# Weight tiles at 128 instead of 64 bytes into their places, and 16 slots that begin 128 bytes later

## The chip, the cores and the metric

The kernel runs on one core of one Trainium2 chip. The metric is the device time of one execution in microseconds (us), the median of several runs; lower is better. Engines are named as in the profile: PE is TensorE's matmul and PEld its weight load, DVE is VectorE, ACT is ScalarE, POOL is GpSimd and SP is SyncE, which here only starts transfers.

## The reference

A decoder trunk of two layers over 512 positions of width 1024, float32 throughout. Layer 0 mixes tokens by retention, layer 1 by an mLSTM; both are followed by a gated feed-forward block with a short causal convolution. Cut to what matters:

```python
def conv_ffn(h, w_up, conv_w, conv_b, w_down):
    u = causal_dwconv(h @ w_up, conv_w, conv_b)
    a, b = jnp.split(u, 2, axis=-1)
    return (jax.nn.silu(a) * b) @ w_down

for i in range(2):
    h = rmsnorm(x, norm_tok_g[i]) * (1.0 + sc_t) + sh_t      # sc, sh, gt from c @ ada_w
    y = retention_mixer(...) if i == 0 else mlstm_mixer(...)   # 4 heads, keys 256, values 512
    x = x + gt_t * y
    h = rmsnorm(x, norm_ffn_g[i]) * (1.0 + sc_f) + sh_f
    x = x + gt_f * conv_ffn(h, ...)                            # inner width 2816
return rmsnorm(x, final_g)
```

Nearly all of the work is matrix products of the 512 positions with weights: the mixers' input and output projections, and the feed-forward block's two.

## The kernel before

**Operands in two parts.** Each float32 operand of a product is split into a high part, rounded to the float32r format, and a low part that holds the rest. A product is three matmuls: high by high, high by low, low by high. So the names come in pairs: `whi` and `wlo` for weights, `hh` and `hl` for the normed input h, `t24h` and `t24l` and `t3h` and `t3l` for sums of its parts, `ggh` and `ggl` for the gated values of the feed-forward block, `yh` and `yl` for a mixer's output, `qkh` and `mqkh` (with an l) for queries and keys, `vh` and `vl` for values, `sh` and `sl` for scores.

**Products.** A matmul loads one operand of 128 columns into the array (PEld) and streams the other through it, 256 or 512 columns wide; while one is streamed the next is loaded. The results are named by their use: `p` are the folded projections, which form four quarter products by seven half-size ones (`fold_pairs`, `folded`), 256 columns wide; `pv` are values, where the input is loaded and the weights are streamed, 256 wide when folded and 512 wide in the first head of each layer; `psc` are scores (keys loaded, queries streamed), `pav` is scores by values (values loaded, scores streamed); `po` are output and down projections, 512 wide, but 256 wide in `boundary`, where a layer half ends and the next one's norm begins; `pf` are the first projections after a norm, 256 wide; `pms` are the means of squares for a norm. `pp` are plain projections, 512 wide.

**Places.** On-chip memory is taken from pools. The pool `slots` has 62 places of 128 partitions by 512 float32 (2,048 bytes each in a partition); all activations lie there. The pool `wpool` has 18 places of 1,024 + `WPAD` float32 (4,352 bytes each) for weights. `WPAD = 64` leaves room for a tile to begin later than its place: tiles of folds, of boundaries and of `ones_d`, which a norm's sums are multiplied with, begin `OFF` float32 into the place (`[:, OFF : OFF + WCOLS]`), those of plain projections begin at 0. `OFF` is 16, which is 64 bytes. In `Beside`, the down projections' weights between the folds, only the last of four low parts is put `OFF` further. A place of `slots` and a place of `wpool` begin alike by 256 bytes: both sizes and the pools' starts are multiples of that.

**Order of the work.** Every instruction is first written down as a call (`Plan.add`), with an estimate of its time and a due time worked back from TensorE's order. `Plan.run` then goes through the engines' clocks and picks for each engine the call that is due first and can start. A tile gets its place when its first writer is picked: the pool's free places are kept in a list sorted by the time at which the place came free, and the first is taken (`room[b.key].pop(0)[1]`). A tile that takes a place over waits on the chip for the last reader of the one before. `Plan.issue` issues everything in this order, so all rows of the profile carry its line, L387, and have to be told apart by their tiles.

**Streams and stages.** Weights come from DRAM by SP's transfers; ACT writes the high part; the low part comes either from DVE (a subtraction) or from ACT and a transfer on POOL that adds (`wlo<-ws`, `wlo<-wt`, `wlo<-raw`). ACT and DVE also read the products out of PSUM, split them, and do the convolutions and norms. The stages by time: conditioning and first projections to about 85 us, retention heads to about 370, boundary and first projections to about 430, feed-forward block to about 705, boundary to about 765, mLSTM heads to about 1090, boundary to about 1150, feed-forward block to about 1430, and the last boundary.

Of the kernel before, what the change touches and what calls it, by code (L numbers as in the profile page):

```python
# [10 lines left out]
F32 = mybir.dt.float32  # L11
F32R = mybir.dt.float32r
# [4 lines left out]
P = 128  # L17
T = 512
# [18 lines left out]
LANDING = (2.5, 3.0)  # L37
LEAD = (4.0, 4.5)
WPAD = 64
OFF = 16  # L40
DIRECT = (0, 0)
ROOT_AT = 1
SPLIT = 4
# [3 lines left out]
NSLOTS = 62  # L47
# [46 lines left out]
class Buf:  # L94


    def __init__(self, pool, shape, dt, tag, name, bufs, psum=False):
        self.args, self.shape, self.key, self.bufs, self.psum = (pool, shape, dt, tag, name), shape, tag, bufs, psum
        self.real, self.uses, self.log, self.at = None, 0, [], ""

    def get(self):
        if self.real is None:
            pool, shape, dt, tag, name = self.args
            self.real = pool.tile(shape, dt, tag=f"{tag}{self.at}", name=name)
        return self.real

# [46 lines left out]
class Plan:  # L153
# [114 lines left out]
    def run(self):  # L268
# [5 lines left out]
        room = {key: [(0.0, i) for i in range(n)] for key, n in KINDS.items()}  # L274
# [32 lines left out]
        def choose(e):  # L307
            cand = []
            for due, n in wait[e]:
                t = start_of(n, free[e])  # L310
                if t is not None:
                    cand.append((due, n, t))
                    if len(cand) == 40:
                        break
            if not cand:
                return None
            soonest = min(t for _, _, t in cand) + 0.02
            for due, n, t in cand:
                if t > soonest:
                    continue  # L320
                end = t + calls[n].occ

                if e == "PE" or not any(d < due and t < t2 < end and d + lag - end < HURRY for d, _, t2 in cand):
                    return t, e, n
            t, n = min((t, n) for _, n, t in cand if t > soonest)
            return t, e, n

        best = {e: choose(e) for e in engines}
        while len(out) < len(calls):
            if not any(best.values()):  # L330
                held = [(calls[n].eng, calls[n].name, [b.args[4] for b in calls[n].bufs])
                        for e in engines for _, n in wait[e][:4]]
                live = [(b.args[4], b.uses) for b in {id(b): b for c in calls for b in c.bufs}.values()
                        if b.bufs and b.log is None and b.uses]
                print(len(live), live)
                raise RuntimeError(f"{len(out)} of {len(calls)}: {[b.args[4] for b in calls[pe[pe_at]].bufs]} {held}")
            t, e, n = min(c for c in best.values() if c)
            c, dirty = calls[n], {e}
            for b in c.bufs:
                if b.log is not None:  # L340
                    b.log, b.busy = None, 0.0
                    if b.bufs:
                        b.at = room[b.key].pop(0)[1]
                        dirty.update(engines)
                        makers[b.key].remove(b.maker)
            occ = c.occ
            if e == "POOL" and c.shared:
                port = (t, t + occ)
            elif e == "DVE" and c.shared:
                occ += SHARE * max(0.0, min(t + occ, port[1]) - max(t, port[0]))  # L350
            if c.fn and c.fn != table:
                table, occ = c.fn, occ + 1.3
            wait[e].remove((c.due, n))
            if e == "PE":
                issued.add(n)
                while pe_at < len(pe) and pe[pe_at] in issued:
                    pe_at, lag = pe_at + 1, t - calls[pe[pe_at]].due
            free[e] = t + occ
            if c.dma:
                dma_free = max(dma_free, t + occ + 1.2) + c.dma  # L360
                c.end = dma_free + LANDING["accum_op" in c.k]
            else:
                c.end = t + occ + c.lat
            for b in c.bufs:
                b.busy = max(b.busy, c.end)
                b.uses -= 1
                if not b.uses and b.bufs:
                    insort(room[b.key], (b.busy, b.at))
                    dirty.update(engines)
            for m, real in c.succs:  # L370
                s = calls[m]
                s.left -= 1
                s.ready = max(s.ready, c.end if real else t + occ)
                if not s.left:
                    dirty.add(s.eng)
                    insort(wait[s.eng], (s.due, m))
            out.append(n)
            self.log.append((t, n, occ))
            for d in dirty:
                best[d] = choose(d)  # L380
# [10 lines left out]
def trunk(ctx: ExitStack, tc: tile.TileContext, xT, cb, pos, vec, ident, decay, zmask, ada, w_s0, w_in0, w_v0,  # L391
          w_o0, w_in1, w_v1, w_f1, w_o1, w_up, w_dn, out):
    nc = tc.nc
    const = ctx.enter_context(tc.tile_pool(name="const", bufs=1))
    slots = ctx.enter_context(tc.tile_pool(name="slots", bufs=1))
    wpool = ctx.enter_context(tc.tile_pool(name="wpool", bufs=1))
    asides = ctx.enter_context(tc.tile_pool(name="asides", bufs=1))
    cond = ctx.enter_context(tc.tile_pool(name="cond", bufs=1))
# [6 lines left out]
    def uid(s):  # L405
        count[0] += 1
        return f"{s}_{count[0]}"

    def tile_of(pool, shape, dt, tag, name):
        return Buf(pool, shape, dt, tag, name, KINDS.get(tag, 0), tag == "ps")  # L410

    def slot(s, dt=F32, w=T):
        return tile_of(slots, [P, w], dt, "s", uid(s))

    def wide(s, dt=F32):
        return tile_of(wpool, [P, WCOLS + WPAD], dt, "w", uid(s))
# [7 lines left out]
    def fixed(pool, shape, dt, name):  # L424
        b = tile_of(pool, shape, dt, name, name)
        b.get()
        return b

    plan = Plan()
    V, A, G, PE, S = (plan.engine(*p) for p in (("DVE", nc.vector), ("ACT", nc.scalar), ("POOL", nc.gpsimd),  # L430
                                                ("PE", nc.tensor), ("SP", nc.sync)))

    V.memset(fixed(const, [P, 32], F32, "pad")[:], 0.0)
    ones = {}
    for name, v in (("d", 1.0 / D), ("v", 1.0 / DV), ("1", 1.0)):
        off = OFF if name == "d" else 0
# [78 lines left out]
    class Chunk:  # L517
        def __init__(self, src, n, off, added=False):
            self.off, self.added = off, added
            self.raw = wide("raw")[:, off : off + n]  # L520
            S.dma_start(self.raw, src)
# [122 lines left out]
                self.p[name] = hi, low_by(name in VADDED)(raw[r], hi, OFF)  # L644

    class Pair:
        def __init__(self, s, w=T):
            self.hi, self.lo = slot(s + "h", F32R, w), slot(s + "l", F32R, w)

        def split(self, src, r=slice(None), eng=None):  # L650
            A.copy(self.hi[:, r], src)
            (eng or V).tensor_tensor(self.lo[:, r], src, self.hi[:, r].bitcast(F32), op=ALU.subtract)

    def pair_of(s, src):
        p = Pair(s)
        p.split(src)
        return p

# [343 lines left out]
    def center_split(v, ps):  # L1002

        t, m = slot("vt"), tile_of(cols, [P, 1], F32, "vm", uid("vm"))
        tf = t[:]
        A.activation(tf, ps[:], AF.Copy, accum_out=m[:])
        G.tensor_scalar(m[:], m[:], -1.0 / DV, None, op0=ALU.mult)
        p = Pair("v")
        A.activation(p.hi[:], tf, AF.Identity, bias=m[:])
        V.scalar_tensor_tensor(p.lo[:], tf, m[:], p.hi[:].bitcast(F32), op0=ALU.add, op1=ALU.subtract)  # L1010
        v.append(p)

    def plain_split(v, ps):
        p = Pair("v")
        p.split(ps[:])
        v.append(p)

# [531 lines left out]
        A.activation(k[:], k[:], AF.Square)  # L1549
        G.tensor_scalar(cos[:], k[:], -2.0, 1.0, op0=ALU.mult, op1=ALU.add)  # L1550

    def rope(p1, p2):
        t = [slot("rp")[:] for _ in range(4)]
        V.tensor_tensor(t[0], p1[:], cos[:], op=ALU.mult)
        V.tensor_tensor(t[1], p2[:], sin[:], op=ALU.mult)
        V.tensor_tensor(t[2], p1[:], sin[:], op=ALU.mult)
        V.tensor_tensor(t[3], p2[:], cos[:], op=ALU.mult)
        V.tensor_tensor(t[0], t[0], t[1], op=ALU.subtract)
        V.tensor_tensor(t[2], t[2], t[3], op=ALU.add)
        return [pair_of("qk", t[n]) for n in (0, 2)]  # L1560

    def half_pair(st, name, finish):

        got = []

        def then(ps):
            got.append(ps)
            if len(got) == 2:
                st[name] = finish(*got)
        return then  # L1570

    h0 = []
# [262 lines left out]
    def conv_then(i, name, kt):  # L1835
        ch = (0 if name == "q" else 8) + i * 2 + kt

        def then(ps):
            acc = slot("mc")[:]
            c = lambda j: col("mcw", j * 16 + ch)  # L1840
            A.activation(acc, ps[:], AF.Identity, bias=col("mcb", ch), scale=c(3))
            for j, s in ((2, 1), (1, 2), (0, 3)):
                V.scalar_tensor_tensor(acc[:, s:], ps[:, : T - s], c(j), acc[:, s:], op0=ALU.mult, op1=ALU.add)
            A.activation(acc, acc, AF.Silu)
            M[i][name].append(pair_of("mqk", acc))
        return then

    def ml_scores(i):
# [224 lines left out]
```

## Time and profile before

| | |
|---|---|
| three runs | 1473.51, 1474.69, 1475.45 us; median 1474.69 |
| the profiled execution, span | 1474.7 us |
| PE busy | 1458.4 us (99%) |
| PEld busy | 1370.7 us (93%) |
| DVE busy | 1289.8 us (87%) |
| ACT busy | 1063.3 us (72%) |
| read from DRAM | 195.29 MB, 134 GB/s over the span |

The profiled execution takes as long as the runs without a profile, so its rows can be set against the median. Busy times of engines overlap. In the rows of groups the last two numbers before the second bar are the group's busy time in us and the mean length of one instruction in ns; a matmul's length holds its way through the array, which overlaps with its neighbours', so its pace is the time of a stretch divided by the count.

### The profile page before, as it was taken

To read this page: it belongs to the slowest core of one execution; us is meant where nothing else is said; L and a number is where in the kernel's file an instruction comes from. 1 tells how busy PE (TensorE), PEld (TensorE's weight loads), DVE (VectorE), ACT (ScalarE), POOL (GpSimd) and SP (SyncE) were. 2 spreads that over 40 slices of the span, in tenths; PEclk is the share of its full clock that TensorE was granted. 3 is DMA by queue.
4 is the path that set the end of the run, shared out by engine and by line. 5 is a ranking of instruction groups with operands and counts; after the bars stand their busy time and mean duration, and the time that the engine had idled before them with its cause. 6 is when DMAs were issued, how large, how long until landed. Compare 5 with 4: busy or idle time off the path is not lost.

```text
span 1474.7 us, 27429 instructions
## 1 busy us (share of the span) xinstructions
PE 1458.4 (99%) x10564; PEld 1370.7 (93%) x10564; DVE 1289.8 (87%) x2183; ACT 1063.3 (72%) x1604; POOL 244.5 (17%) x279
## 2 busy tenths in 40 slices
PE   8999999999999999999999999999999999999998
PEld 7889999998999999989999998999989999999997
DVE  7899988887998888889897999999989988886866
ACT  5578768786588676666678985988856877667673
POOL 0313112112011111110001321222121011101010
PEclk8999999999999999999999999999999999999999
DMA  9868988988598999799457875888877678568661
GB/s 365 250 165 218 275 232 234 242 251 208 152 223 210 269 266 253 214 236 248 145 176 172 211 207 183 198 194 196 253 190 193 165 183 206 155 168 206 171 162 59
DMA packets 90822, 306.16 MB, mean 208 GB/s; under 512 B 11954, under 2 KB 14514, under 8 KB 90691
## 3 DMA queue, kind: packets, MB, share of 16 engines
q0 software_dynamic: 29520, 106.97, 38.6%
q1 hardware_dynamic: 60882, 197.18, 38.6%
q8 instruction: 82, 1.34, 0.4%
q10 hardware_dynamic: 288, 0.27, 0.1%
q14 instruction: 50, 0.40, 0.1%
HBM read 195.29 MB, written 2.12 MB: 134 GB/s over the span
## 4 chain that ended last, share of the span: by engine, by line
PE 49%; DMA 1%; ACT 1%; DVE 1%; issue 1%; DVEq 0%; POOL 0%; POOLq 0%
PE p L387 20%; PE po L387 16%; PE pv L387 5%; PE pf L387 3%; PE pav L387 2%; DMA wlo<-wt 1%; PE psc L387 1%; ACT whi L387 0%; PE pp L387 0%; ACT mc L387 0%; DVE sl L387 0%; DVE mc L387 0%; ACT wlo L387 0%; ACT L387 0%; DVE ws L387 0%
## 5 line engine op out<-in xcount | busy, mean ns | idle before, releaser
L387 PE MATMUL p<-hh,whi 128*128 128x256 f32 (+1 forms) x1029 | 284.7, 278 | 1.6 <-DVE p L387 1.5
L387 PE MATMUL p<-hl,whi 128*128 128x256 f32 x1024 | 283.6, 277 | 0.0
L387 PE MATMUL p<-hh,wlo 128*128 128x256 f32 x1024 | 281.6, 278 | 0.1
L387 ACT ACTIVATE wlo<-whi 128x1024 fp32r<-128x1024 f32 (+1 forms) x205 | 215.4, 1055 | 25.6 <-PE po L387 14.7
L387 PEld LDWEIGHTS p<-hh,whi 128*128 128x128 f32 x1029 | 193.9, 188 | 3.0 <-DVE p L387 2.4
L387 PEld LDWEIGHTS p<-hl,whi 128*128 128x128 f32 x1024 | 192.5, 188 | 0.4
L387 PEld LDWEIGHTS p<-hh,wlo 128*128 128x128 f32 x1024 | 191.4, 188 | 0.5 <-DMA wlo<-ws 0.3
L387 PE MATMUL p<-t24h,whi 128*128 128x256 f32 x768 | 170.4, 279 | 2.1 <-ACT fs L387 2.1
L387 PE MATMUL po<-ggl,whi 128*128 128x512 f32 (+1 forms) x448 | 153.1, 343 | 0.0
L387 PE MATMUL po<-ggh,whi 128*128 128x512 f32 (+1 forms) x448 | 152.0, 344 | 0.7 <-ACT whi L387 0.7
L387 PE MATMUL po<-ggh,wlo 128*128 128x512 f32 (+1 forms) x448 | 152.5, 343 | 0.0
L387 PE MATMUL p<-t24l,whi 128*128 128x256 f32 x512 | 142.1, 277 | 0.0
L387 DVE SCALAR_TENSOR_TENSOR x<-po,mod,x 128x512 f32<-128x512 f32 (+1 forms) x184 | 113.6, 628 | 30.7 <-PE po L387 29.8
L387 ACT CAST whi<-raw 128x1024 fp32r<-128x1024 f32 (+1 forms) x113 | 113.5, 1015 | 32.6 <-PE po L387 8.4
L387 PEld LDWEIGHTS p<-t24h,whi 128*128 128x128 f32 x768 | 130.4, 188 | 4.9 <-ACT fs L387 2.5
L387 DVE SCALAR_TENSOR_TENSOR cv<-p,vecs,cv 128x511 f32<-128x511 f32 (+1 forms) x152 | 111.2, 743 | 12.0 <-ACT cv L387 11.7
L387 DVE SCALAR_TENSOR_TENSOR ada<-ada,c_ext 128x1025 f32<-128x1025 f32 x96 | 117.6, 1227 | 0.3 <-DMA ada<-ada 0.3
L387 PE MATMUL po<-yl,whi 128*128 128x256 f32 (+1 forms) x352 | 115.3, 328 | 0.0
L387 PE MATMUL po<-yh,whi 128*128 128x256 f32 (+1 forms) x354 | 115.3, 328 | 0.0
L387 PE MATMUL po<-yh,wlo 128*128 128x256 f32 (+1 forms) x352 | 115.3, 328 | 0.0
L387 POOL DMA_DIRECT2D wlo<-wa x55 | 47.5, 864 | 366.3 <-ACT wlo L387 207.7
L387 ACT CAST whi<-ws 128x1024 fp32r<-128x1024 f32 x88 | 92.0, 1048 | 20.7 <-DVE ws L387 13.6
(292 smaller groups left out, 4394.6 us busy)
## 6 DMA issues: line engine op xcount, KB each, us to landing
ada<-ada SPq DMA_DIRECT2D x96, 512.5 KB, 6.6
wlo<-ws POOLq DMA_DIRECT2D x61, 512.0 KB, 7.6
wlo<-wa POOLq DMA_DIRECT2D x55, 512.0 KB, 6.5
wlo<-wt POOLq DMA_DIRECT2D x45, 512.0 KB, 7.5
wa<-w_up SPq DMA_DIRECT2D x38, 512.0 KB, 5.6
wb<-w_up SPq DMA_DIRECT2D x38, 512.0 KB, 8.9
wlo<-raw POOLq DMA_DIRECT2D x34, 512.0 KB, 8.2
raw<-w_o SPq DMA_DIRECT2D x32, 512.0 KB, 7.8
```

The source lines that it names most:

```text
L387: getattr(c.obj, c.name)(*[real(v) for v in c.a], **{key: real(v) for key, v in c.k.items()})
```

## The change

`OFF` becomes 32 float32, 128 bytes. Of the 62 slots the last 16 (`SHIFTED`) come from a pool of their own, `shifted`, that lies behind a gap of 32 float32 (`SHIFT`), so that they begin 128 bytes later by 256; a second gap of 32 float32 behind them brings the later pools back to multiples of 256. POOL fills both gaps once at the start.

Which place a tile of `slots` gets is now decided by `place`, among the places that are free at that time by the planner's clock: keys and values (`likes=True`) take a shifted place if there is one, all other split pairs (`likes=False`) a plain one if there is one; any other tile takes a shifted one while more than 9 (`SPARED`) of them are free, and else a plain one. If the preferred kind has none, the other is taken. Within a kind the place that came free first is taken. Tiles of other pools get their places as before.

```diff
-OFF = 16
+OFF = 32
+SHIFTED = 16
+SPARED = 9
+SHIFT = 32
@@ class Buf
     def get(self):
         if self.real is None:
             pool, shape, dt, tag, name = self.args
+            if self.shifted and self.at >= NSLOTS - SHIFTED:
+                pool = self.shifted
             self.real = pool.tile(shape, dt, tag=f"{tag}{self.at}", name=name)
@@ Plan.run
+        def place(b, t):
+
+            free_at = room[b.key]
+            if b.key != "s":
+                return free_at.pop(0)[1]
+            open_at = [i for f, i in free_at if f <= t + 1e-9]
+            shifted = [i for i in open_at if i >= NSLOTS - SHIFTED]
+            plain = [i for i in open_at if i < NSLOTS - SHIFTED]
+            if b.likes is None:
+                first = shifted if len(shifted) > SPARED else plain
+            else:
+                first = shifted if b.likes else plain
+            i = (first or shifted or plain)[0] if open_at else free_at[0][1]
+            free_at.remove(next(f for f in free_at if f[1] == i))
+            return i
...
-                        b.at = room[b.key].pop(0)[1]
+                        b.at = place(b, t)
@@ trunk
     slots = ctx.enter_context(tc.tile_pool(name="slots", bufs=1))
+    gap = ctx.enter_context(tc.tile_pool(name="gap", bufs=1))
+    shifted = ctx.enter_context(tc.tile_pool(name="shifted", bufs=1))
+    gap2 = ctx.enter_context(tc.tile_pool(name="gap2", bufs=1))
     wpool = ctx.enter_context(tc.tile_pool(name="wpool", bufs=1))
...
-    def slot(s, dt=F32, w=T):
-        return tile_of(slots, [P, w], dt, "s", uid(s))
+    def slot(s, dt=F32, w=T, likes=None):
+        b = tile_of(slots, [P, w], dt, "s", uid(s))
+        b.likes, b.shifted = likes, shifted
+        return b
...
+    G.memset(fixed(gap, [P, SHIFT], F32, "gap_in")[:], 0.0)
+    G.memset(fixed(gap2, [P, 64 - SHIFT], F32, "gap_out")[:], 0.0)
...
     class Pair:
-        def __init__(self, s, w=T):
-            self.hi, self.lo = slot(s + "h", F32R, w), slot(s + "l", F32R, w)
+        def __init__(self, s, w=T, likes=False):
+            self.hi, self.lo = slot(s + "h", F32R, w, likes), slot(s + "l", F32R, w, likes)
...
-        p = Pair("v")
+        p = Pair("v", likes=True)
...
-        return [pair_of("qk", t[n]) for n in (0, 2)]
+        return [pair_of("qk", t[n], keys) for n in (0, 2)]
...
-            M[i][name].append(pair_of("mqk", acc))
+            M[i][name].append(pair_of("mqk", acc, name == "k"))
```

More of the change, by code (lines that the diff above doesn't have):

```diff
@@ L99, in __init__ @@
         self.real, self.uses, self.log, self.at = None, 0, [], ""
+        self.likes, self.shifted = None, None
     def get(self):
@@ L652, in split, with pair_of @@
             (eng or V).tensor_tensor(self.lo[:, r], src, self.hi[:, r].bitcast(F32), op=ALU.subtract)
-    def pair_of(s, src):
-        p = Pair(s)
+    def pair_of(s, src, likes=False):
+        p = Pair(s, likes=likes)
         p.split(src)
@@ L1013, in plain_split @@
     def plain_split(v, ps):
-        p = Pair("v")
+        p = Pair("v", likes=True)
         p.split(ps[:])
@@ L1550, in rope_tables, with rope @@
         G.tensor_scalar(cos[:], k[:], -2.0, 1.0, op0=ALU.mult, op1=ALU.add)
-    def rope(p1, p2):
+    def rope(p1, p2, keys):
         t = [slot("rp")[:] for _ in range(4)]
@@ L1568, in then @@
             if len(got) == 2:
-                st[name] = finish(*got)
+                st[name] = finish(*got, name == "k")
         return then
```

## The prediction

> **What bounds the kernel now.** I read the page's busy times first, then the groups by form, the chain of waits in order of time, the busy time by stretch, and the waits.
>
> ```profile
> span 1474.7 us, 27429 instructions
> PE 1458.4 (99%) x10564; PEld 1370.7 (93%) x10564; DVE 1289.8 (87%) x2183; ACT 1063.3 (72%) x1604; POOL 244.5 (17%) x279
> PEclk8999999999999999999999999999999999999999
> ```
>
> The span is 1474.7 us and the median of the three runs 1474.69, so the sum below is made against 1474.7 and nothing lies around it. TensorE is idle for 1474.7 - 1458.4 = 16.3 us only, at a full clock after the first slice. So its pace per product sets the time, and this pace isn't constant. In the chain of waits (start, length, what, count) equal products stand with two paces:
>
> ```profile
> 688.96 12.72 DMA wlo<-wt
> ...
> 710.94 19.08 PE po L387 x162
> 746.51 19.32 PE pf L387 x164
> 771.29 21.76 PE pv L387 x96
> 844.19 11.31 PE pv L387 x96
> 855.95 8.16 PE pv L387 x72
> 1133.88 15.99 PE pf L387 x141
> 1434.12 18.81 PE po L387 x166
> ```
>
> Length over count: po 117.8 ns at 711 but 113.3 at 1434; pf 117.8 at 747 but 113.4 at 1134; pv, two stretches of one stage in a row, 117.8 and then 113.3. These are products of 256 columns. The pv at 771 are 512 wide and take 226.7 = 2 x 113.3, so 113.3 ns per 256 columns is the pace of the streamed operand alone, and 4.45 ns are lost in each slow product. A long stretch is all of one pace or all of the other: a pace, once taken, holds. The groups by form show the same in the mean length of one matmul (the last ns before the bar). First three short windows: po from 711 to 729, po from 1435 to 1452, pv from 844.5 to 855:
>
> ```profile
> L387 PE MATMUL po<-ggl,whi 128*128 128x256 f32 x53 | 14.5, 281 | 0.0
> ...
> L387 PE MATMUL po<-ggl,whi 128*128 128x256 f32 x51 | 13.7, 276 | 0.0
> ...
> L387 PE MATMUL pv<-whi,hl 128*128 128x256 f32 x23 | 6.4, 280 | 0.0
> ```
>
> Then the whole span:
>
> ```profile
> L387 PE MATMUL p<-hh,whi 128*128 128x256 f32 x1024 | 284.5, 278 | 1.6 <-DVE p L387 1.5
> L387 PE MATMUL p<-hl,whi 128*128 128x256 f32 x1024 | 283.6, 277 | 0.0
> L387 PE MATMUL p<-hh,wlo 128*128 128x256 f32 x1024 | 281.6, 278 | 0.1
> L387 PE MATMUL p<-t24h,whi 128*128 128x256 f32 x768 | 170.4, 279 | 2.1 <-ACT fs L387 2.1
> ...
> L387 PE MATMUL p<-t24l,whi 128*128 128x256 f32 x512 | 142.1, 277 | 0.0
> ...
> L387 PE MATMUL pv<-whi,hl 128*128 128x256 f32 x192 | 53.3, 278 | 0.0
> ...
> L387 PE MATMUL pv<-whi,hl 128*128 128x512 f32 x32 | 12.5, 389 | 0.0
> ...
> L387 PE MATMUL pav<-sl,vh 128*128 128x256 f32 x64 | 17.9, 282 | 0.2 <-DVE sl L387 0.2
> ...
> L387 PE MATMUL psc<-mqkh,mqkl 128*128 128x256 f32 x16 | 4.5, 282 | 0.0
> ...
> L387 PE MATMUL pms<-ssh,ones_d 128*128 128x256 f32 x7 | 1.9, 278 | 0.0
> ```
>
> 281 ns goes with the long pace, 276 with the short one. The view has 39 groups of 256 columns, `p<-hh,whi` the first and `pms<-ssh` the last, with 8,422 products. The first five rows, 4,352 products, have a weighted mean of 277.8, so (277.8 - 276) / 5, about 36%, are slow. The rows are rounded to 1 ns, which moves this by a tenth; I take 32%. That is 0.32 x 8,422 x 4.45 ns = **12.0 us**, all that the two paces can be worth.
>
> **Which products are slow.** Places follow from the code. A slot is 2,048 bytes and a weight tile 4,352 = 17 x 256, so all begin alike by 256 bytes, and only the offset in a tile decides. Before, in each pair of a loaded operand and the one streamed meanwhile: p, pf, po at boundaries and pms lie 64 bytes apart, pv (where weights are streamed) 64 bytes the other way, psc and pav 0 apart. The rows: 0 apart is always slow (282, 282); 64 either way has both paces. So the distance matters at 0, and no row has 128.
>
> **The change, part by part.**
> (1) *Offset 64 to 128 bytes.* The instructions, their sizes and their count stay; what moves is the distance of every p, pf, boundary po, pms and pv, from 64 to 128 bytes. Unknown, so bounded. Best: none is slow, -12.0 us less the part of psc and pav (below). Worst: 128 acts as 0 does, all 8,422 slow: (8,422 x 0.68) x 4.45 = +25.5 us. I take the better side: if 0 is the bad distance and places repeat by 256 bytes, 128 is the furthest from it, and 64, half way, has a third slow. I assume that a third of the loss stays, because stalls still put stretches into the long pace: -8 us.
> (2) *The last 16 of 62 slots begin 128 bytes later, keys and values are put there first.* That takes psc and pav from 0 to 128. There are 192 pav and 96 psc products of 256 columns; at 282 they lose (282 - 276) x 4.45 / 5 = 5.3 ns each, 1.5 us, part of the 12.0. But a query, a score, an h or a t24 that finds no plain slot goes to the shifted ones, where its distance to a weight is 0. x takes shifted slots first (while more than 9 are open), so 46 plain ones must hold h and its sums (16 + 8 + 4) and gg or y. I count +0.5 us, between 0 and +2 (4% of 8,422 going from fast to slow is 1.5).
> (3) *A place is chosen by kind, no longer the one that is free longest.* The planner takes only places that are free by its own clock, so the order of the instructions stays. But a tile may now follow its last user more closely, and the writer waits for the reader. The nearest price is a stall of today:
>
> ```profile
> PE p L387 <- ACT fs L387: 2.1, 2, 1.1
> PE pst L387 <- DMA x<-xT: 1.5, 1, 1.5
> PE p L387 <- DVE p L387: 1.5, 3, 1.0
> ```
>
> One is 0.5 to 1.5 us; I take +0.5, from 0 to +3, and below 0 nothing since no place comes free earlier. Behind such a writer (DVE or ACT) its engine's queue stands, and TensorE for the tile.
> (4) *Two small memsets on POOL at the start.* At 128x32 they lie between these two:
>
> ```profile
> 0.24 0.10 POOL L2064 MEMSET const-float32-0.0<- 128x1 f32 x1 [0.24 <-issue]
> ...
> 0.74 0.52 POOL L387 MEMSET warm<- 128x512 f32 x1 [0.29 <-POOLq L2064]
> ...
> 7.68 3.60 PE L387 MATMUL pst<-x,ones 128*128 128x256 f32 x8 [1.52 <-DMA x<-xT]
> ```
>
> so 0.2 to 1.0 us, possibly ahead of the warm tile. TensorE then waits 1.52 us for x at 7.68 anyway: 0. Without that cover, +0.3.
>
> **Where the gain meets other engines.** The stretches (length, then busy times) that hold products of the long pace, and last one of the short:
>
> ```profile
> 85.00:160.00 75.00, 73.85 (x583) 71.89 (x582) 70.78 (x118) 59.90 (x100) 16.92 (x23) 1.00 0.84 219
> 235.00:305.00 70.00, 70.00 (x580) 68.71 (x580) 60.54 (x101) 56.29 (x88) 15.13 (x18) 1.00 0.84 214
> 705.00:765.00 60.00, 60.00 (x512) 60.00 (x511) 55.03 (x114) 36.28 (x66) 2.60 (x3) 1.00 0.49 141
> 835.00:905.00 70.00, 70.00 (x518) 66.75 (x517) 65.72 (x103) 56.28 (x88) 17.79 (x18) 1.00 0.75 207
> 905.00:1000.00 95.00, 95.00 (x735) 91.56 (x734) 91.47 (x140) 79.33 (x121) 25.26 (x28) 1.00 0.80 192
> 1205.00:1440.00 235.00, 235.00 (x1715) 220.45 (x1714) 185.95 (x297) 162.15 (x228) 29.30 (x34) 1.00 0.70 174
> ```
>
> Order: PE, weight loads, DVE, ACT, POOL, clock, DMA. The clock is 1.00 at either pace, so it is not the cause. From 705 to 765 all 512 are slow, 2.3 us, and DVE has 5.0 us free: this goes through. From 85 to 160 and from 835 to 1000 DVE is busy 94 to 96%; there a faster TensorE waits for VectorE. I let three quarters of the 8 through: -6.0. **Sum:** -6.0 + 0.5 + 0.5 = -5.0, so 1474.7 - 5.0 = **1469.7 us**; its own range is 1461 to 1472.
>
> **A rule that speaks against it.** The rows show 117.8 against 113.3 ns for one shape at one clock. The Trainium skill (page "SBUF — State Buffer", section "Who interferes with whom") says that TensorE has two independent read ports, one for the streamed operand and one for weight loads, and waits on nobody. By that rule no distance matters and the gain is 0. The trace agrees only in part: pav and psc at distance 0, always slow, speak against it, but they are also short groups mixed with other widths.
>
> **The rivals.**
> (a) *The distance does nothing*: the paces come from how a stretch begins (stalls, changes of width), and pav is slow from its mix. For it: pv goes from slow to fast in one stage at one distance. Against: 282 in every psc and pav row. Then (1) gives 0, (3) gives 0 to +1: 1475.
> (b) *VectorE takes over*: the long pace goes, but DVE at 94 to 96% keeps the pace in the head stages; what is left is 705 to 765 (2.3 us) and the feed-forward parts, less the 1.0: about 1473.
> (c) *Slower: the paces are dealt anew, and worse.* The long slow stretch from 711 on follows a stretch of the chain that hangs on a DMA (688.96) and holds until the 512-wide pv of 771. With other waits at other places stretches such as pf at 1134 or the 235 us from 1205 to 1440 can come to keep the long pace. It decides from 32% slow products on; at 50% it costs 0.18 x 8,422 x 4.45 = +6.7, with (2) and (3) 1482. For it: 64 bytes has both paces, 128 may as well. Against: nothing in the rows says that 128 is worse.
> (d) *128 acts like 0* (places repeat by 128 bytes): +25.5, 1500. For it: no row has 128, and 64 either way looks the same in pace. Against: slow po is 281 long and slow pv, 64 the other way, 280; the two sides would be alike if places repeated by 128. That is 1 ns, so weak.
>
> **How the numbers follow.** The forecast has a chance of 0.50, (a) 0.12, (b) 0.11, (c) 0.18, (d) 0.09. Under 0.2% (2.9 us) a measurement of this kernel can't tell a change from none. The forecast gives 0.49 faster; (b) 0.05 faster, the rest same; (a) 0.08 same, 0.02 faster, 0.02 slower; (c) 0.17 slower, 0.01 same; (d) 0.09 slower. With 0.01 of the forecast to same that is faster 0.56, same 0.16, slower 0.28. The range is 1462 to 1487: below it the case that all 12.0 and more goes through, above it (d) and the worst of (c). The likeliest case's own range, 1461 to 1472, stands beside it.
>
> **What would show it.** Right: the 256-column groups fall to 276 or 277, psc and pav with them; the chain's po and pf at 711 to 765 show 113.3 per product; TensorE's idle time grows by 2 to 4 us, with VectorE as releaser. (1) is wrong if po, pf or p stay at 278 or above; (2) is wrong if psc and pav stay at 282, or if p rows split between the two values by stage; (3) if new waits of over 1 us stand for a slot's writer; (4) if the first real product comes later than 7.68. A mean of 281 in all groups would mean (d).

## The result: slower, and the profile after

The changed kernel took 1511.9 us (median of four runs, 1510.3 to 1513.9) beside 1475.1 us for the kernel before (four runs, 1473.5 to 1478.3): 2.5% slower, ratio 1.0251 with a 95% interval of 1.0234 to 1.0268. The forecast was 1469.7 us, with a range of 1462 to 1487. The profiled execution has a span of 1510.1 us, 35.4 us more than the 1474.7 before. The first lines of its page:

```profile
span 1510.1 us, 27447 instructions
PE 1494.9 (99%) x10564; PEld 1405.4 (93%) x10564; DVE 1295.2 (86%) x2183; ACT 1067.6 (71%) x1604; POOL 242.8 (16%) x281
PEclk9999999999999999999999999999999999999999
```

The same 10,564 matmuls keep TensorE busy for 1494.9 - 1458.4 = 36.5 us longer, and its idle time falls from 16.3 to 1510.1 - 1494.9 = 15.2 us. So the whole loss is in the pace of the products, none of it in waits, at a full clock. Put down to the 8,422 products of 256 columns alone, it is 36.5 / 8,422 = 4.3 ns for each. The groups by form of the same kernel (the last ns before the bar is the mean length of one matmul):

```profile
L409 PE MATMUL p<-hh,whi 128*128 128x256 f32 x1024 | 289.6, 283 | 0.7 <-DVE p L409 0.7
...
L409 PE MATMUL pv<-whi,hl 128*128 128x256 f32 x192 | 54.1, 282 | 0.0
...
L409 PE MATMUL pav<-sl,vh 128*128 128x256 f32 x64 | 17.8, 281 | 0.0
...
L409 PE MATMUL pv<-whi,hl 128*128 128x512 f32 x32 | 12.5, 389 | 0.0
...
L409 PE MATMUL psc<-mqkh,mqkl 128*128 128x256 f32 x16 | 4.5, 281 | 0.0
```

p went from 278 to 283, the 256-wide pv from 278 to 282. psc and pav, from 282 to 281, hardly moved, though keys and values get a place at the new distance wherever one is free. The 512-wide pv kept 389, but this row says nothing of 128 bytes: its weights begin at place 0 in both kernels, as those of all plain projections do. It shows that a wide product does not feel distance 0: it keeps the prediction's 226.7 ns, 113.3 per 256 columns, where narrow products at distance 0 take up to 120.0 (below). The chain of waits (start, length, what, count) shows it stretch by stretch:

```profile
725.00 19.44 PE po L409 x162
...
860.82 11.52 PE pv L409 x96
872.81 8.54 PE pv L409 x72
...
1220.34 8.63 PE p L409 x72
```

Length over count: po 120.0 ns (117.8 before), the two pv stretches 120.0 and 118.6 (117.8 and 113.3 before), p in a fold of the second feed-forward block 119.9. There are again two paces, but now 118.6 and 120.0, and no stretch shown has 113.3. Two of the prediction's stretches, by windows (length, then busy times in its order). The changed kernel comes to the same work later, by 14 us at the first (po x162 at 725.00, before 710.94) and by 26 us at the second (the chain's p at 1220.34, before 1194.67), so the windows are moved by as much:

```profile
719.00:779.00 60.00, 60.00 (x502) 60.00 (x502) 54.66 (x113) 36.21 (x65) 2.60 (x3) 1.00 0.48 141
...
1231.00:1466.00 235.00, 235.00 (x1646) 220.54 (x1645) 182.02 (x288) 157.03 (x220) 28.07 (x33) 1.00 0.68 170
```

In the 60 us from 719 on TensorE gets through 502 matmuls instead of 512, in the 235 us from 1231 on through 1,646 instead of 1,715 (a part of this is that the end of the window meets other widths), though it is busy for all of the time in both kernels. VectorE is not the bound in the second: it is busy 182 of 235 us. TensorE's largest waits:

```profile
PE p L409 <- ACT fs L409: 2.2, 3, 0.9
PE pst L409 <- ACT hh L409: 1.8, 1, 1.8
```

One of them (`ACT hh`, 1.8 us) is not among those quoted of before, where a wait for `x<-xT` (1.5 us) stood; their sum is no larger, as the idle time says.

### The profile page after: what moved, and what is told of

Same layout as the page of the kernel before. It is cut to its first block, busy times and chain, and to the rows that moved or that the text cites. A ratio compares the mean times of both kernels' runs of the same rounds, so it can differ in the third digit from the quotient of the medians.

```text
span 1510.1 us, 27447 instructions
## 1 busy us (share of the span) xinstructions
PE 1494.9 (99%) x10564; PEld 1405.4 (93%) x10564; DVE 1295.2 (86%) x2183; ACT 1067.6 (71%) x1604; POOL 242.8 (16%) x281
## 4 chain that ended last, share of the span: by engine, by line
PE 93%; DMA 2%; DVE 2%; issue 1%; ACT 1%; SPq 0%; DVEq 0%; POOL 0%; POOLq 0%; ACTq 0%
PE p L409 40%; PE po L409 27%; PE pv L409 9%; PE pf L409 5%; PE pav L409 4%; PE pp L409 3%; PE pst L409 2%; PE psc L409 2%; DMA wb<-w_up 1%; PE pc L409 1%; DMA wlo<-ws 1%; DMA raw<-w_s 1%; ACT whi L409 0%; DMA x<-xT 0%; DVE ada L409 0%
## 5 line engine op out<-in xcount | busy, mean ns | idle before, releaser
L409 PE MATMUL p<-hh,whi 128*128 128x256 f32 (+1 forms) x1029 | 289.8, 283 | 0.7 <-DVE p L409 0.7
L409 PE MATMUL p<-hl,whi 128*128 128x256 f32 x1024 | 289.1, 283 | 0.0
L409 PE MATMUL p<-hh,wlo 128*128 128x256 f32 x1024 | 285.7, 282 | 0.5 <-DMA wlo<-ws 0.5
L409 PE MATMUL p<-t24h,whi 128*128 128x256 f32 x768 | 175.0, 283 | 2.9 <-ACT fs L409 1.7
L409 ACT CAST whi<-raw 128x1024 fp32r<-128x1024 f32 (+1 forms) x113 | 113.9, 1015 | 37.4 <-PE po L409 8.7
L409 DVE SCALAR_TENSOR_TENSOR x<-po,mod,x 128x512 f32<-128x512 f32 (+1 forms) x184 | 113.4, 627 | 30.4 <-PE po L409 29.6
L409 DVE SCALAR_TENSOR_TENSOR ada<-ada,c_ext 128x1025 f32<-128x1025 f32 x96 | 118.3, 1234 | 0.9 <-DMA ada<-ada 0.9
L409 ACT COPY fs<-p 128x256 f32<-128x256 f32 x154 | 57.0, 370 | 72.7 <-PE p L409 70.4
```

The costliest lines, as they stand in the source:

```text
L409: getattr(c.obj, c.name)(*[real(v) for v in c.a], **{key: real(v) for key, v in c.k.items()})
```

## The experiments

The theory after the result: the pace of a 256-column product is set by the distance, modulo 256 bytes, from the operand that is streamed to the one that is loaded meanwhile, and 128 bytes is a bad distance. (The first expectations below say that places repeat by 128 bytes; the scan of all distances speaks for 256.) The rivals: the loss comes from the 16 shifted slots, or from how the stretches begin, as rival (a) had it.

### The pace by distance, alone

A kernel of matmuls only. 48 products of 256 columns in a row, the streamed operand at a multiple of 1,024 bytes, the loaded one at a place that goes from 0 to 256 in steps of 16; each such stretch three times: after one 16-column product (a), after six 512-wide ones (b), after 24 products at distance 0 (c).

```diff
+for p in PLACES:                       # 0, 16, ... 256 bytes
+    short("short")
+    stretch(f"a{p}after_short", p, 48) # loads w[:, p // 4 + k * 128 : ... + 128], streams 256 columns
+for p in PLACES:
+    wide("wide", 6);          stretch(f"b{p}after_wide", p, 48)
+for p in PLACES:
+    stretch("zero", 0, 24);   stretch(f"c{p}after_zero", p, 48)
```

> Not the trunk: 2,448 products of 256 columns plus the leads, where the loaded operand lies 0 to 256 bytes (in steps of 16) after the streamed one, 48 products a stretch; each distance is met three times, after one short product, after six 512-wide ones, after 24 products at distance 0. The output is left at zero. Theory (places repeat by 128 bytes, so 128 and 256 are as bad as 0): took 281 to 283 at 0, 128 and 256 in all three, 276 at 64 and 192 after a short product. Rival (places repeat by 256, 128 is bad for another reason, such as the new places of slots): 276 at 128. What 16 to 48 bytes give is open; if one of them is 276 after all three leads, it is a better offset than 64.

The chain of waits of this kernel (start, length, stretch, count):

```profile
14.12 5.85 PE a0after_short L53 x48
...
37.32 5.55 PE a64after_short L53 x48
...
60.30 5.86 PE a128after_short L53 x48
...
83.68 5.75 PE a192after_short L53 x48
...
113.97 5.75 PE b0after_wide L53 x48
...
142.31 5.66 PE b64after_wide L53 x48
...
170.59 5.77 PE b128after_wide L53 x48
...
304.09 5.69 PE c128after_zero L53 x48
...
338.39 5.44 PE c192after_zero L53 x48
```

At distance 0 a stretch takes 5.85 us after a short product and 5.75 after wide ones; I take the 0.10 as what the short product adds at the start. Less that, 0 has (5.85 - 0.10) / 48 = 119.8 and 5.75 / 48 = 119.8 ns; 64 has (5.55 - 0.10) / 48 = 113.5 after short and 117.9 after wide; 128 has 120.0, 120.2 and, after zero, 118.5; 192 after zero has 113.3, but after short 117.7, where the short pace was expected. So with no slots, no stalls and no other engine at work, distance alone moves the pace from 113.3 to 120, 128 is as bad as 0 or nearly so, and 64 and 192 have both paces, by what came before them. Both long paces of the changed kernel, 118.6 and 120.0, are here.

The Trainium skill (page "SBUF — State Buffer", section "Who interferes with whom") gives TensorE two independent read ports and has it wait on nobody. The prediction took from it that there is one pace at any distance; these rows show one shape at one clock, with no other engine busy beside it, at 113.3 or 120 ns by place alone. The measurement decides. Whether it is these two reads that get in each other's way is not shown.

### The change in two halves, and distance 0 for all

The offset of 128 bytes without the slots, in the kernel before:

```diff
-OFF = 16
+OFF = 32
```

> The kernel before with weight tiles at 128 bytes and nothing else; scores and values stay at distance 0. Theory (the distance of 128 costs): 1505 to 1512, all groups of 256 columns at 281 to 283. Rival (the choice of places of the slots costs, by waits or by spilled tiles): 1470 to 1478.

1511.4 us (median of 1509.3, 1509.7 and 1513.2), ratio 1.0245 (1.0223 to 1.0266), as the theory expected. A fourth execution, the profiled one, was disturbed as a whole (6758.8 us) and is left out; no rows are read from it, so the expected mean lengths stay unseen here. This one line gives the whole loss; the slots beside it add nothing that can be told (1511.9 with them).

The other half, the slots without the offset, in the changed kernel:

```diff
-OFF = 32
+OFF = 16
```

> The changed kernel with weight tiles back at 64 bytes: slots, places and choice as changed. Theory: 1470 to 1479, p, po, pf and pv at 277 to 279 as before, psc and pav (now at 128) at 281 to 282 as before. Rival (the choice of places costs): 1500 or more.

1482.5 us (1478.8 to 1483.6), ratio 1.0047 (1.0033 to 1.0062): a small loss of their own, above the 1470 to 1479 that the theory expected and far below the rival's 1500. Its page has this line of busy times:

```profile
PE 1462.9 (99%) x10564; PEld 1370.7 (93%) x10564; DVE 1292.5 (87%) x2183; ACT 1064.7 (72%) x1604; POOL 242.5 (16%) x281
```

Two of its groups by form:

```profile
L409 PE MATMUL po<-ggl,whi 128*128 128x256 f32 x192 | 53.2, 281 | 0.0
...
L409 PE MATMUL pav<-sl,vh 128*128 128x256 f32 x64 | 17.8, 280 | 0.0
```

One stretch of its chain, the po of the last boundary:

```profile
1439.66 19.55 PE po L409 x166
```

And TensorE's largest waits (total, times, longest):

```profile
PE pst L409 <- ACT hh L409: 2.8, 3, 1.7
PE p L409 <- ACT fs L409: 2.6, 4, 1.0
```

With a span of 1481.8 us TensorE is busy 4.5 us longer than before and idle for 18.9 us, 2.6 more. The waits for `hh` and `fs` are each larger in total than any of those quoted of before, as step (3) feared. And a stretch that had the short pace of distance 64 before (18.81 us at 1434.12 in the prediction) has the long one now, 19.55 / 166 = 117.8, so that `po<-ggl` has 281 in all of its products. It stands in a run of 288 such products, which is 288 x 4.45 ns = 1.3 of the 4.5 us; the mean lengths of p, pf and pv stay at 277 to 280, and no run places the rest. pav is at 280 to 281 and psc at 281 to 282, one or two ns less than before of the six that step (2) hoped for.

Distance 0 for p, pf, boundary po, pms and pv, in the kernel before:

```diff
-OFF = 16
+OFF = 0
```

> The kernel before with weight tiles at 0 bytes, so that every product is at distance 0. Theory (places repeat by 128 bytes): as long as with 128, 1505 to 1512, mean lengths equal to those after within 1 ns. Rival (128 has a price of its own): off by more than 5 us from it, 1495 to 1503 if all go at 117.8 ns.

1513.8 us (two runs, 1513.5 and 1514.0), ratio 1.0266 (1.0243 to 1.0288). Groups of this kernel:

```profile
L387 PE MATMUL p<-hh,whi 128*128 128x256 f32 x1024 | 290.2, 284 | 2.2 <-DVE p L387 2.1
...
L387 PE MATMUL pv<-whi,hl 128*128 128x256 f32 x192 | 54.2, 283 | 0.0
```

284 and 283, one ns above the changed kernel, and 2 us longer. So 0 is bad for these groups too, by the same size, and the slots' distance is not needed for it.

### 192 bytes, and a short product ahead

The first kernel gave 113.3 ns at 192 after zero, and 113.5 at 64 after a short product. Both were tried in the kernel before, the second by a 16-column product ahead of each fold pair and of the boundary stretches behind the feed-forward blocks:

```diff
-OFF = 16
+OFF = 48
```

> The kernel before with weight tiles at 192 bytes, so that p, po, pf and pms lie where pv lay and pv where they lay. Theory (64 either way has both paces, 128 and 0 one): 1465 to 1495, groups of 256 columns at 277 to 280. Rival (any later beginning than 64 costs, as a tile that crosses more lines would): 1505 or more.

```diff
 # fold_pairs
-                  lead and not n)
+                  True)
 # boundary
-            for u, run in last:
-                item([u], lambda w, run=run, p=p, after=after: run(w[0], *HALVES[p], after), False)
+            for n, (u, run) in enumerate(last):
+                item([u], lambda w, run=run, p=p, n=n, after=after: run(w[0], *HALVES[p], after,
+                                                                        lead=p + n == 0 and not late), False)
```

> The kernel before, with one more 16-column product of no use ahead of every pair of folded projections and ahead of the boundaries after the feed-forward blocks (14 more or so; before, five folds or boundaries had one). Theory (a short product at 64 sets the short pace, as in all seven places of before): p and the po and pf from 705 to 765 come to 276 to 277, gain 5.4 us (half of the p excess and all of the 2.3 us) less 14 x 0.1 us, so 1467 to 1472. Rival (the pace is chance): within 2 us of before, and stretches behind a short product at either pace.

Both missed. 192 bytes took 1499.4 us (1498.3 to 1500.5), ratio 1.016 (1.0138 to 1.0182), 4 us over the expected range, though the mean lengths of p, po, pf and pv (277 to 280) are in theirs. A group and a stretch of its chain:

```profile
L387 PE MATMUL p<-hh,whi 128*128 128x256 f32 x1024 | 286.2, 280 | 1.5 <-DVE p L387 1.4
```

```profile
1146.04 16.62 PE pf L387 x141
```

The pf is at 16.62 / 141 = 117.9 ns, where before it was at 113.4, and p has a mean length of 280, which at this distance goes with the long pace: by the starts of the products in the trace, 90% of p and practically all of pf and of the narrow po are over 115.5 ns apart. So 192 holds the long pace in the kernel, though a bare stretch of it can hold the short one. pv, which lies at 64 here, keeps 278.

The short products, 25 more than before (10,589 matmuls instead of 10,564; the expectation counted 14), gave 1482.9 us (1481.0 to 1484.1), ratio 1.0048 (1.0032 to 1.0064). The po behind the two feed-forward blocks, in the chain of this kernel:

```profile
714.05 19.08 PE po L387 x162
...
1439.76 19.55 PE po L387 x166
```

The first still has the long pace, 117.8 ns, that it was to lose. The second has it too, where before it had the short one. By the starts of the products in the trace, of the 32 stretches that now follow a 16-column product 13 run at 113.3 to 113.7 ns and 19 at 117.7 to 118.3; the seven of before were all short. That is what the rival said of the stretches, but not of the time, which is 7.7 us longer than before and not within 2. What sets the short pace in a bare stretch doesn't set it in the kernel. Why the lead failed was asked of a second kernel of matmuls only: at 64 and at 192, eight leads and none, each after 24 products at distance 0 and after six wide ones; then single distances from 52 to 76 and from 180 to 204.

```diff
+for p in (64, 192):
+    for name, lead in leads.items():   # none, one short product of 16 to 192 columns, two, one or three wide
+        stretch("zero", 0, 24);  lead(p);  stretch(f"d{p}z_{name}_x", p, 36)
+    for name, lead in leads.items():
+        wide("wide", 6);         lead(p);  stretch(f"d{p}w_{name}_x", p, 36)
```

> Not the trunk: stretches of 36 products of 256 columns at distance 64 and 192, each after 24 products at distance 0 or after six 512-wide ones and then one of nine leads (none, a short product of 16, 64, 128 or 192 columns, one at distance 0, two of 16, one or three 512-wide ones), and stretches at 52 to 76 and 180 to 204 bytes in steps of 4. The output is left at zero. Theory (the pace is a rhythm that what comes before sets, only possible near 64 and 192): 113.3 ns at 64 after a short product of 16, 117.8 without; some other lead gives 113.3 at 192. Rival (any distance over 48 and under 80 has the short pace, and chance decides): no lead decides it.

Its chain of waits at 64, after zero (z): a 16-column lead at the stretch's own place (`s`), the same lead at place 0 (`s16at`); then after wide (w) the same two leads:

```profile
24.10 4.34 PE d64z_s_x L53 x36
...
31.33 4.20 PE d64z_s16at_x L53 x36
...
86.47 4.20 PE d64w_s_x L53 x36
...
92.07 4.34 PE d64w_s16at_x L53 x36
```

Less the 0.10 of a lead, 4.34 us are 117.8 ns a product and 4.20 are 113.9. The same lead gives the long pace after one history and the short one after the other, and the place of the lead turns this around. So at 64 the pace depends on the state that the work before has left, and the theory "a short product sets the short pace" falls. At 192 it has a lead that gives 113.3, as expected: after 24 products at distance 0 or after three wide ones a stretch takes 4.08 us, while a single short product leaves it long. In the kernel the work ahead of a fold pair differs from pair to pair.

### All distances, and the kernel at 76 bytes

If 64 goes either way, is there a distance that goes one way? A third kernel of matmuls only takes all distances from 0 to 256 in steps of 4, each stretch of 32 after zero (a), after wide (b) and after short (c).

> Not the trunk: 32 products of 256 columns at each distance from 0 to 256 bytes in steps of 4, after 16 products at distance 0, after five 512-wide ones and after one of 16 columns. The output is left at zero. Theory (128 and 0 hold only the long pace; a few distances hold the short one, and some of them take it up from any lead): 281 to 284 at 0, 128 and 256 in all three, 277 or less in some of the three at 64 and 192, in all three at 52 and 76. Rival (128 is bad by the kernel's data or places alone): 276 at 128.

Its chain of waits:

```profile
17.42 3.84 PE a0after_zero L53 x32
...
206.41 3.68 PE a52after_zero L53 x32
...
235.06 3.81 PE a60after_zero L53 x32
...
249.71 3.77 PE a64after_zero L53 x32
254.63 3.65 PE b64after_wide L53 x32
...
293.17 3.64 PE a76after_zero L53 x32
...
487.32 3.84 PE b128after_wide L53 x32
...
714.88 3.63 PE a192after_zero L53 x32
...
758.07 3.92 PE a204after_zero L53 x32
763.16 3.63 PE b204after_wide L53 x32
...
947.32 3.84 PE a256after_zero L53 x32
```

3.84 / 32 is 120.0, 3.63 is 113.4, and 3.68 is 115.0, a stretch whose first products still have the long pace. Few distances reach the short pace, and they don't lie around 128: 52 and 76 after all three beginnings, 64 and 88 after some of them, and, as their mirror images (256 less these), 192, 180, 168 and 204 after some. These lie 12 bytes apart; 60, between two of them, has 3.81. The rest take between 3.70 and 3.88 after zero. A good place can be the worst one too: 204 has 113.4 ns after wide, but after zero 3.92 / 32 = 122.5, the longest after zero of all 65 distances. 256 takes what 0 takes, and 192 is not 64, so places repeat by 256 and not by 128 bytes, as far as distances up to 256 show, and 128 lies between the two good sets with most of the other places.

The kernel before with 76 bytes:

```diff
-OFF = 16
+OFF = 19
```

> The kernel before with weight tiles at 76 bytes. Theory (76 takes up the short pace from any lead, and its counterpart for pv, 180, mostly holds the long one): p, po, pf at 276 (7,000 x 1.2 ns = -8 us), pv at 280 (1,000 x 2.4 ns = +2): 1467 to 1471. Rival (76 and 64 are alike in a long run, or transfers to places off 64 bytes cost): 1473 or more.

1474.3 us (1472.3 to 1475.6) beside 1476.0, ratio 0.9988 (0.9973 to 1.0003): not to be told from before, and short of the 1467 to 1471 expected. The busy times on its page:

```profile
PE 1455.6 (99%) x10564; PEld 1366.1 (93%) x10564; DVE 1290.5 (88%) x2183; ACT 1063.2 (72%) x1604; POOL 243.3 (17%) x279
```

Three of its groups by form:

```profile
L387 PE MATMUL p<-hh,whi 128*128 128x256 f32 x1024 | 283.5, 277 | 2.0 <-DVE p L387 1.7
...
L387 PE MATMUL pv<-whi,hl 128*128 128x256 f32 x192 | 53.4, 279 | 0.0
...
L387 PE MATMUL po<-ggl,whi 128*128 128x256 f32 x192 | 52.2, 276 | 0.0
```

Here the scan does carry over: po is at 276 (281 in its slow stretch before) and p at 277. But pv, which lies at 180 the other way round, went to 279, so TensorE is busy only 2.8 us less, and its idle time is 1.6 us more (1473.5 - 1455.6 = 17.9 us), in one profiled execution of each.

### Two offsets

pv should come to the good distance as well: the weights of folded values at 180, all others at 76. Modulo 256, pv's loaded operand then lies 76 from its streamed one.

```diff
-OFF = 16
+OFF = 19
+OFFV = 45
@@ class ValueFold
-                raw[name] = wide("wv")[:, OFF : OFF + WCOLS]
+                raw[name] = wide("wv")[:, OFFV : OFFV + WCOLS]
...
-                hi = high_part(raw[r], OFF)
+                hi = high_part(raw[r], OFFV)
```

> The kernel before with weight tiles at 76 bytes, those of folded values, which are streamed, at 180, so that p, po, pf, pms and pv are all at 76. Theory (76 takes up the short pace from any lead): all these groups at 276, 4 us less than with 76 alone (1,000 pv at 113.5 rather than 117.3), of which VectorE's queue takes a part: 1469 to 1473. Rival (the shorter products only wait longer for VectorE and transfers): within 1.5 us of the kernel before, TensorE's idle time up by what the products lose.

1478.0 us (1475.3 to 1480.8), ratio 1.0022 (1.0013 to 1.0031): a little slower, where 1469 to 1473 was expected. The group of pv:

```profile
L388 PE MATMUL pv<-whi,hl 128*128 128x256 f32 x192 | 54.6, 285 | 0.0
```

285 is longer than this group has at any distance tried before it in the kernel (283 at 0). So 76 as such is not the whole of it. In the scan only the loaded operand was moved off a multiple of 256; in pv it is the streamed one, and that may count by itself. Another reading is not excluded: that 76, like 204 in the scan, has a state that is worse than any bad place, and pv met it. No run tells the two apart.

The last two keep pv at 64, as before, and put all others at 76 or at 52 (`OFFV = 16` with `OFF = 19` or `OFF = 13`).

> The kernel before with weight tiles at 76 bytes, but those of folded values at 64 as before. Theory (the short pace is held where the loaded operand is moved; streamed weights are best left alone): p, po and pf at 276 to 277, pv at 278, so 1.5 us less than with 76 for all, 1470 to 1474, ratio 0.996 to 0.999. Rival (the gain is taken by waits for VectorE and transfers): ratio 0.999 to 1.002.

> The same with 52 bytes in place of 76. Theory (52 took up the short pace from any lead too): the same time as with 76 within 1.5 us, p, po and pf at 276 to 278. Rival (the scan's few products a stretch say little of a long run): p at 279 or more, 1477 or more.

76 with 64: 1475.5 us, ratio 1.0002 (0.999 to 1.0013), as the rival said. 52 with 64: 1477.4 us, ratio 1.0025 (1.0012 to 1.0037), 1.9 us more than 76, and pf at 278 to 279: 52 holds the short pace less well. No version beats the kernel before. Where the gain went with 76 and 64, by windows of this kernel:

```profile
235.00:305.00 70.00, 67.94 (x554) 66.45 (x553) 57.91 (x97) 54.83 (x85) 15.12 (x18) 0.98 0.81 208
705.00:765.00 60.00, 59.99 (x529) 59.79 (x529) 56.01 (x115) 36.82 (x66) 2.61 (x3) 1.00 0.53 156
```

TensorE's largest wait from 235 to 305 us:

```profile
PE p L388 <- DMA wlo<-wa: 1.8, 1, 1.8
```

From 705 to 765 it gets through 529 products instead of 512, the gain that the pace promised. From 235 to 305 it gets through 554 instead of 580: TensorE, which had no idle time there before, now has 70.00 - 67.94 = 2.06 us of it, 1.8 for one weight's transfer, and the granted clock there is 0.98 instead of 1.00. At the rate of each window before (70.00 / 580 = 0.121 and 60.00 / 512 = 0.117 us a product) the 26 lost are 3.1 us and the 17 won 2.0. Over the whole span TensorE is busy 1457.3 us and idle for 16.9, that is 1.1 us less and 0.6 more than before, so the gain is lost inside its busy time too. By the starts of the 256-wide products in the trace, those that follow 116.5 to 121.5 ns behind the one before (the long pace) cost 5.3 us less than before, counted from 113.35 ns a product, and those that follow more than 150 ns behind (too long for any pace) 4.9 us more. Why these became more, and why the clock was lower there, is not shown.

## Why the prediction was wrong, point by point

**The bound.** Right: TensorE's pace sets the time. It was 99% busy before and after, and 36.5 us more of busy time against 1.1 us less of idle time are the whole result.

**The two paces and the reading by distance.** Right in kind: 0 is bad, 64 has both. The bare stretches show it, and the kernel at offset 0 shows it for the kernel's own p and pv. The third of slow products fits too: by the starts in the trace of before it is about 30%. Incomplete in size: the long pace of 64, 117.8 ns, was taken for the only one. At 0 and 128 it is 118.6 to 120.0.

**Step (1), the offset.** Here the prediction failed. It had both bounds, -12.0 and +25.5 us, and took the better side with "if 0 is the bad distance and places repeat by 256 bytes, 128 is the furthest from it, and 64, half way, has a third slow". Places do repeat by 256, but the pace doesn't improve smoothly away from 0: the good places are a few points around 52 to 88 and their mirror images. The rows had 64 at its best and its worst and nothing at 128, so that a curve was drawn through two known places. -8 us was forecast for this step; TensorE was busy 36.5 us longer, at paces of 118.6 to 120.0 ns, and the offset alone took the kernel to 1511.4 us.

**The bound +25.5 itself** was too small, as a term: 8,422 x 0.68 products at + 4.45 ns. All of them were indeed slow, but by more: the 4.3 ns that each product lost come on top of the 0.32 x 4.45 = 1.4 of before, so the mean stands 5.7 to 5.8 above the short pace, 4.45 + 1.3. The 1.3 ns also hit the 32% that were slow already: 8,422 x 1.3 = 11 us, and 25.5 + 11 = 36.5. The 1.3 ns are worked back from the 36.5, but the paces bear them out: 118.6 and 120.0 are 0.8 and 2.2 above 117.8. That is the missing part of rival (d), which gave 1500.

**Rival (d)** was the right case, at 0.09, with a wrong reason. It said that places repeat by 128 bytes. They don't: 64 and 192 differ in the bare stretches after the same beginning (117.9 and 113.3 ns after zero). 128 is simply outside the good set. The sign named for it, a mean of about 281 in all groups, is what came (280 to 284).

**Step (2), the slots.** psc and pav were to gain 1.5 us by going from 0 to 128. They went from 282 to 281: 128 is a long place for them as well, so most of the 1.5 did not come. The spilled tiles can't be told apart beside it.

**Step (3), the choice of places.** Priced at +0.5 (0 to +3). With the offset the idle time fell by 1.1 us in all, so nothing of it shows there. Its sign, a new wait of over 1 us, was met by `hh` (1.8 us), but the kernel with the short products, which has no slots of this kind, waits 1.8 us for `hh` as well. With the offset of before (the slots alone) idle time rose by 2.6 us, inside the bound, and TensorE's busy time by 4.5 us, which the step did not have: 1.3 of it is a stretch that took the long pace at 64. That is rival (c) on a small scale.

**Step (4), the memsets.** Nothing, as said: TensorE's first wait, for the warm tile, is 1.3 us in both kernels. The first product with x starts at 7.9 us instead of 7.68, but so it does in the kernel at offset 0, which has no such memsets.

**VectorE as the next bound.** Three quarters of a gain were to come through. The kernel at 76 bytes bears out that a part is lost: 2.8 us less busy time, 1.6 us more idle time. It does not bear out that VectorE is what takes it: the waits for its `p` grew from 1.5 to 1.9 us only, and the others stand for ACT (`whi` 1.2 us, `hh` 1.0) and for transfers of weights.

**The Trainium skill's rule and rival (a).** Both would have left the time as it was. The bare stretches, without stalls, speak against both: distance alone moves the pace. But (a) had a point, since at 64 what ran ahead of a stretch decides which of the two paces it takes.

**What stays open.** Why these places are good or bad, and what the state is that work leaves behind. A clash between the reads of the loaded and of the streamed operand would fit that it is the narrow products that lose, but no run separates the two reads. That the start of the streamed operand counts by itself rests on one kernel and has a rival there.

## What to carry to other kernels

When a profile shows two paces for one shape at one clock, look at where the operands begin, and measure the places in a bare loop of that shape before choosing one: all distances in steps of 4 bytes fitted into one kernel of 961 us here. Try each place after several kinds of work: 192, good after some, was bad in the kernel, and 76, good after all three tried, was good there for p, po and pf. Bound an unknown place by its worst case and price that case at the worst pace, not at the one at hand. A pace that is won in a tight kernel need not show in its time: here 17 products won in one stage stood beside 26 lost in another, with a wait for a transfer and a lower clock.

## What the runs showed of the hardware that was not expected

- The pace of 256-column float32r products with a load for each depends on where the operands begin: 113.3 ns at best, 120.0 at distance 0, with 256 the same as 0, and 122.5 in one stretch at 204. Products of 512 columns at distance 0 don't show it (226.7 ns, 113.3 per 256 columns).
- The good places of the loaded operand are single points, 12 bytes apart (52, 64, 76, 88 and, mirrored, 204, 192, 180, 168); a few bytes beside them the pace is long again (3.81 us for 32 at 60, between 3.68 at 52 and 3.64 at 76). Only 52 and 76 were short after all three beginnings.
- At some places both paces hold steadily, and which one is taken depends on the products before: one 16-column product switched it (4.20 or 4.34 us for 36), in a direction that depends on what ran ahead of it. In the kernel 13 of 32 stretches behind such a product were short and 19 long.
- 76 bytes is good for one way round (`po`, 276 ns in mean length); the same distance modulo 256 with a shifted streamed operand gave the longest mean length of these products in the kernel (`pv`, 285).
